# Moving the decode state updates of a gated linear attention from TensorE matmuls in the heads to VectorE multiply-adds in the MLPs

## The chip, the cores and the metric

The kernel runs on one core of one Trainium2 chip. The metric is the device time of one execution in microseconds, and the median of three runs is compared. What counts is the whole step, from the first load to the last output.

## The reference, cut to what matters

One inference step of a two-layer decoder: 256 prompt tokens and 8 decode sequences of 8 new tokens (320 rows together), width 2048, float32. Layer 0 mixes tokens with a gated linear attention (GLA) of 4 heads (keys 256, values 512), layer 1 with a spatial gating unit (gMLP). Each is followed by a layer norm and by a dense MLP of width 8192 with a squared ReLU, and by another layer norm. The part that the change touches is the new state of each decode sequence and head, an output of its own:

```python
def step(s, inp):                     # one chunk; for a decode sequence: its 8 tokens
    qi, ki, vi, gi = inp
    b = jnp.cumsum(gi, axis=-2)
    b_last = b[..., -1:, :]
    k_to_end = ki * jnp.exp(b_last - b)
    ...
    s_new = (jnp.exp(b_last[..., 0, :])[..., None] * s
             + jnp.einsum('bhsk,bhsv->bhkv', k_to_end, vi))
    return s_new, o                   # o uses the old s
def sq_relu_mlp(x, w1, w2):
    return jnp.square(jax.nn.relu(x @ w1)) @ w2
x = layer_norm(ALPHA * x + mixer(x), ...)
x = layer_norm(ALPHA * x + sq_relu_mlp(x, ...), ...)
```

There are 32 such states (8 sequences by 4 heads), each 256 by 512 in float32 (512 KB). Nothing else in the step reads `s_new`.

## The kernel before, in words

**Units.** All activations stand transposed in SBUF, features on partitions, 320 token columns. Every large product goes through `group` (line 165), which walks weight *units* of 512 input rows by 256 output columns. `unit` (line 129) loads a unit (512 KB) on SyncE's queue, ScalarE rounds it to `wh` (line 144, "cast") and VectorE subtracts to get the rest `wl` (line 145, "split"); `mm3` (lines 158 to 163) then issues three matmuls of 320 columns for each of 4 row blocks and 2 column blocks, 24 per unit. Units alternate between two rings of buffers, `a` (4 buffers) and, once the heads are done, `b` (4 buffers, line 712), so a cast waits until TensorE has finished the unit that had its buffer, 8 units earlier. There are 736 units: 24 in each of 4 heads, 32 for the GLA output product, 256 for the first MLP, 64 and 32 for the gMLP layer, 256 for the second MLP.

**Heads.** `Head` (lines 343 to 674) projects v, k, q and the gate of one head, and runs the attention in steps that are spread over the units (`Side`). `ev_v` (line 469) and `ev_k` (line 423) lay each decode token out in four copies of rounded parts and rests, which vector transposes and small gathers (GpSimd's queue, line 341) bring into row order. `sample_step` (line 620) takes one sequence and one half of the keys: two matmuls for the outputs with the old state (line 631), one matmul `pu` of k by v (line 634, 512 columns), and on VectorE `st = st * dec + pu` (line 635); after the second half GpSimd's queue stores the state (line 638). The old state is loaded on SyncE's queue (line 612).

**Norms.** `residual_gemm` (line 853) adds a product to the residual `z` and takes the statistics in `Norm.take` (line 758). The sums over partitions are two pairs of matmuls with a matrix of ones (`total`, lines 754 and 755); `close` (line 801) turns them into mean and `rstd` (lines 806 to 808, and `rsqrt`, lines 186 to 190), and `apply` (line 812) normalises the 16 feature tiles: VectorE lines 816 and 817, ScalarE lines 819 and 820, VectorE line 822 for the rest `yl`. `gemm_of` (line 842) starts the next product on the raw residual `dgh`, `dgl` (two column groups, 8 units, corrected afterwards), so that TensorE needs the first normalised tile only 8 units after the residual product has ended.

**MLPs.** `mlp` (line 875) runs four times a product with `w1`, squared ReLU (VectorE lines 887 and 889, ScalarE lines 888 and 893), and a product with `w2` (VectorE line 908). 

**Order.** Each engine runs its own instructions strictly in the order in which they were built. That order is not the order of the code alone: the program is built with a scheduler that places each instruction on its engine as soon as it reckons its inputs ready, within the buffers that the pools have.

Of the kernel before, what the change touches and what calls it, by code (L numbers as in the profile page):

```python
# [8 lines left out]
F32 = mybir.dt.float32  # L9
F32R = mybir.dt.float32r  # L10
# [65 lines left out]

@with_exitstack
def step_kernel(ctx: ExitStack, tc: tile.TileContext, A):
# [44 lines left out]
    cp.tile([P, LINE - 8], F32, tag="fill", name="fill")  # L123
# [159 lines left out]
    kz = gp.tile([P, 4, 2, 2, P], F32R, tag="kz", name="kz")  # L283
    nc.gpsimd.memset(kz[:].bitcast(F32), 0.0)

# [57 lines left out]
    class Head:  # L343
# [25 lines left out]
        def gate_logits(hd):  # L369

            hd.dec = g2.tile([P, 2, NCH + DB], F32, tag="dec", name=nm("dec"))
# [51 lines left out]
        def ev_k(hd, kt, ps):  # L423
# [12 lines left out]
            kst = g2.tile([P, DB, 4, DS], F32, tag="vst", name=nm("kst"))  # L436
            two = [P, DB, 2, DS]
            hi = kst[:, :, 0:2, :]
            nc.scalar.copy(hi.bitcast(F32R), bc4(kte[:, TP:T]).to_broadcast(two))
            nc.vector.tensor_sub(kst[:, :, 2:4, :], bc4(kte[:, TP:T]).to_broadcast(two), hi)  # L440
# [8 lines left out]
        def gather_kz(hd, q):  # L449
            kb = hd.kb[:].rearrange("p a b -> p (a b)")  # L450
            gather(kz[:, q].bitcast(F32).rearrange("p k b f -> p (k b f)"), kb[:, 2 * TP :], q, nc.gpsimd)
# [17 lines left out]
        def ev_v(hd, vt, ps):  # L469
# [5 lines left out]
            two = [P, DB, 2, DS]  # L475
            hi = vst[:, :, 0::2, :]
            nc.scalar.copy(hi.bitcast(F32R), bc4(ps[:, TP:T]).to_broadcast(two))
            nc.vector.tensor_sub(vst[:, :, 1::2, :], bc4(ps[:, TP:T]).to_broadcast(two), hi)
# [141 lines left out]
        def sample_step(hd, b, kt):  # L620
# [9 lines left out]
            for part in (stl, sth):  # L630
                nc.tensor.matmul(po[:], qm[:, kt, b * P : (b + 1) * P], part[:], start=False,  # L631
                                 stop=(b == DB - 1 and kt == 1 and part is sth))
            pu = gltile()
            nc.tensor.matmul(pairs(pu), kz[:, i, kt, g, :], hd.v_sample(g), start=True, stop=True)  # L634
            nc.vector.scalar_tensor_tensor(st[:, kt, :], st[:, kt, :], hd.dec[:, kt, NCH + b : NCH + b + 1],
                                           pu[:], op0=ALU.mult, op1=ALU.add)
            if kt == 1:
# [516 lines left out]
```

## Time and profile before

| what | value |
|---|---|
| median of 3 runs | 2691.23 us (2691.22 to 2691.33) |
| span of the profiled execution | 2689.4 us, 1.8 us under the median: what lies around the span |
| TensorE busy | 2680.7 us |
| VectorE busy | 1550.3 us (58%) |
| ScalarE busy | 1162.5 us (43%) |
| GpSimd busy | 226.4 us (8%) |
| granted TensorE clock, mean | 1.000 |
| DMA | 442.42 MB, 165 GB/s on average |

Matmuls are pipelined: a matmul of 320 columns shows 0.31 us from its start to its end, but the next one starts 0.14 us later. Busy shares of TensorE therefore say that it never stopped, and what an extra matmul costs is read from starts, not from durations. The heads end about 445 us into the span; the first MLP runs from about 545 to 1430 us, the second from about 1780 to 2667 us.

### The profile page before, as it was taken

The page shows a single profiled execution, that of the slowest core. Times are in us where ns is not written, and L with a number is a line of the kernel's source. Part 1 is how long each engine was busy: PE and PEld are TensorE (multiplying, and loading weights), DVE is VectorE, ACT ScalarE, POOL GpSimd, SP SyncE. Part 2 cuts the span into 40 slices and gives each one's busy share as a digit, 9 for nine tenths or more (in the row PEclk, how much of TensorE's full clock was granted, in tenths as well). Part 3 has the DMA queues.
Part 4 walks back from the last instruction along what each step waited for, and adds up shares of the span by engine and source line. Part 5 has one row for each costly group of instructions (what it writes and reads, how often), then busy time and mean ns, then how long its engine had stood idle before and what let it go on. Part 6 is the DMA issues. An engine that isn't in the chain of part 4 may idle for free.

```text
span 2689.4 us, 44906 instructions
## 1 busy us (share of the span) xinstructions
PE 2680.7 (100%) x18395; PEld 2658.8 (99%) x18395; DVE 1550.3 (58%) x2322; ACT 1162.5 (43%) x1638; POOL 226.4 (8%) x391
## 2 busy tenths in 40 slices
PE   9999999999999999999999999999999999999999
PEld 9999999999999999999999999999999999999998
DVE  7677677885444444444478776686444444444446
ACT  5455455564334334333446554355334333333434
POOL 4353341000000000000001032000000000000000
PEclk9999999999999999999999999999999999999999
DMA  8667667545445545444445555455445444454552
GB/s 252 220 196 249 217 198 253 189 142 159 155 150 155 151 150 156 150 153 152 150 152 161 157 158 149 134 165 153 153 150 156 150 152 154 150 155 150 152 154 79
DMA packets 138494, 442.42 MB, mean 165 GB/s; under 512 B 20912, under 2 KB 27952, under 8 KB 138288
## 3 DMA queue, kind: packets, MB, share of 16 engines
q1 hardware_dynamic: 121440, 408.08, 49.2%
q0 software_dynamic: 16304, 30.82, 3.7%
q8 instruction: 144, 2.36, 0.4%
q10 hardware_dynamic: 544, 0.66, 0.1%
q14 instruction: 62, 0.51, 0.1%
HBM read 409.60 MB, written 22.02 MB: 160 GB/s over the span
## 4 chain that ended last, share of the span: by engine, by line
PE 99%; DMA 0%; ACT 0%; DVE 0%; ACTq 0%; issue 0%; DVEq 0%
PE mm L161 32%; PE mm L163 32%; PE mm L162 31%; PE gl L631 1%; PE gl L634 1%; PE gl L589 1%; PE gl L1003 0%; PE gl L573 0%; DMA raw<-gla_w_in 0%; ACT z L1087 0%; DMA xr<-xT 0%; PE gl L558 0%; PE gl L603 0%; PE gl L574 0%; PE gl L552 0%; PE gl L1004 0%
## 5 line engine op out<-in xcount | busy, mean ns | idle before, releaser
L145 DVE TENSOR_TENSOR wl<-raw,wh 128x1024 fp32r<-128x1024 f32 (+1 forms) x740 | 902.3, 1220 | 953.2 <-ACT wh L144 950.9
L144 ACT CAST wh<-raw 128x1024 fp32r<-128x1024 f32 (+1 forms) x740 | 771.5, 1044 | 1251.9 <-PE mm L163 1127.1
L163 PE MATMUL mm<-yh,wh 128*128 128x320 f32 x2624 | 805.9, 307 | 0.0
L161 PE MATMUL mm<-yh,wl 128*128 128x320 f32 x2624 | 803.2, 309 | 0.0
L162 PE MATMUL mm<-yl,wh 128*128 128x320 f32 x2624 | 794.9, 303 | 0.0
L161 PE MATMUL mm<-hh,wl 128*128 128x320 f32 x2048 | 631.5, 308 | 0.0
L163 PE MATMUL mm<-hh,wh 128*128 128x320 f32 x2048 | 629.0, 307 | 0.0
L162 PE MATMUL mm<-hl,wh 128*128 128x320 f32 x2048 | 619.9, 303 | 0.0
L162 PEld LDWEIGHTS mm<-yl,wh 128*128 128x128 f32 x2624 | 492.7, 188 | 0.0
L163 PEld LDWEIGHTS mm<-yh,wh 128*128 128x128 f32 x2624 | 491.4, 187 | 0.0
L161 PEld LDWEIGHTS mm<-yh,wl 128*128 128x128 f32 x2624 | 491.0, 188 | 0.0
L161 PEld LDWEIGHTS mm<-hh,wl 128*128 128x128 f32 x2048 | 384.6, 188 | 0.0
L162 PEld LDWEIGHTS mm<-hl,wh 128*128 128x128 f32 x2048 | 384.6, 188 | 0.0
L163 PEld LDWEIGHTS mm<-hh,wh 128*128 128x128 f32 x2048 | 383.4, 187 | 0.0
L161 PE MATMUL mm<-xh,wl 128*128 128x320 f32 x768 | 238.2, 311 | 1.4 <-DVE wl L145 0.7
L163 PE MATMUL mm<-xh,wh 128*128 128x320 f32 x768 | 236.4, 309 | 0.0
L162 PE MATMUL mm<-xl,wh 128*128 128x320 f32 x768 | 235.2, 306 | 0.0
L161 PEld LDWEIGHTS mm<-xh,wl 128*128 128x128 f32 x768 | 144.1, 188 | 5.4 <-DVE wl L145 1.0
L162 PEld LDWEIGHTS mm<-xl,wh 128*128 128x128 f32 x768 | 144.3, 188 | 4.4 <-issue 1.2
L163 PEld LDWEIGHTS mm<-xh,wh 128*128 128x128 f32 x768 | 143.7, 187 | 2.6 <-issue 0.7
L1053 POOL CAST ident_r<-ident 128x128 fp32r<-128x128 f32 x1 | 0.3, 286 | 1027.9 <-PE gl L772 1027.9
L936 POOL DMA_DIRECT2D bsp<-sg_wT x1 | 0.6, 558 | 999.7 <-PE mm L163 999.7
(265 smaller groups left out, 2380.3 us busy)
## 6 DMA issues: line engine op xcount, KB each, us to landing
raw<-mlp_w SPq DMA_DIRECT2D x512, 512.0 KB, 3.5
raw<-gla_w_in SPq DMA_DIRECT2D x94, 512.0 KB, 4.1
raw<-sg_w_in SPq DMA_DIRECT2D x64, 512.0 KB, 3.6
st<-state SPq DMA_DIRECT2D x32, 512.0 KB, 5.7
o_state_s<-st POOLq DMA_DIRECT2D x32, 512.0 KB, 4.2
raw<-gla_w_out SPq DMA_DIRECT2D x32, 512.0 KB, 4.5
raw<-sg_w_out SPq DMA_DIRECT2D x32, 512.0 KB, 3.5
va<-blk POOLq DMA_DIRECT2D x128, 32.0 KB, 4.3
```

What stands on the lines that cost most here:

```text
L144: nc.scalar.copy(hi[:, ks, :], raw[:, ks, :])
L145: nc.vector.tensor_sub(lo[:, ks, :], raw[:, ks, :], hi[:, ks, :].bitcast(F32))
L161: nc.tensor.matmul(ps, wl[:, kk, s], x_h, start=first, stop=False)
L162: nc.tensor.matmul(ps, wh[:, kk, s], x_l, start=False, stop=False)
L163: nc.tensor.matmul(ps, wh[:, kk, s], x_h, start=False, stop=last)
L589: nc.tensor.matmul(pairs(pu), hd.ktp[:, kt, blk, :], hd.v_prompt(blk), start=(blk == 0), stop=(blk == 1))
L631: nc.tensor.matmul(po[:], qm[:, kt, b * P : (b + 1) * P], part[:], start=False, stop=(b == DB - 1 and kt == 1 and part is sth))
L634: nc.tensor.matmul(pairs(pu), kz[:, i, kt, g, :], hd.v_sample(g), start=True, stop=True)
L936: nc.gpsimd.dma_start(wsT, A["sg_wT"])
L1053: nc.gpsimd.tensor_copy(ident_r[:], ident[:])
```

## The change

The state update leaves the heads. The one matmul per step, its VectorE instruction, the store, and the row-ordered copies of k (`kz`, with their gathers) are gone; the load of the old state stays, since the outputs need it. Instead the kernel keeps the scaled keys (`ks_all`) and decays (`dec_all`) of all heads in SBUF, writes v of the decode tokens to DRAM (`v_dram`, 16 issues on GpSimd's queue), and computes the states in the MLPs, 16 in each: GpSimd's queue loads the old state again into the only buffer `su` (line 856 of the new file), ScalarE scales its two halves by the decay (line 862), and for each of 8 tokens a row of v (2 KB) is read from DRAM into all 128 partitions (`vt`, two buffers, 256 KB, line 851), and VectorE runs two multiply-adds `su = vt * ks + su` over 128 by 512 (line 872). After the eighth token GpSimd's queue stores the state (line 875). `Spread` is to spread these steps over the MLP's units in the code. Ring `b` has 3 buffers instead of 4.

```diff
+class Spread:
+    def __init__(self, steps, units):
+        self.steps, self.units, self.done, self.called = list(steps), units, 0, 0
+    def __call__(self):
+        self.called += 1
+        while self.done < len(self.steps) and self.done * self.units < self.called * len(self.steps):
+            self.steps[self.done]()
+            self.done += 1
...
+    ks_all = cp.tile([P, H, 2, DB * DS], F32, tag="ks", name="ks_all")
+    dec_all = cp.tile([P, H, 2, NCH + DB], F32, tag="dec", name="dec_all")
+    v_dram = dr.tile([H, 2, P, 4, P], F32, tag="v", name="v_dram")
-    kz = gp.tile([P, 4, 2, 2, P], F32R, tag="kz", name="kz")
-    nc.gpsimd.memset(kz[:].bitcast(F32), 0.0)
...
-            nc.scalar.copy(hi.bitcast(F32R), bc4(kte[:, TP:T]).to_broadcast(two))
-            nc.vector.tensor_sub(kst[:, :, 2:4, :], bc4(kte[:, TP:T]).to_broadcast(two), hi)
+            nc.scalar.copy(ks_all[:, hd.h, kt, :], kte[:, TP:T])
-            nc.vector.transpose(hd.kb[:, 2 + kt, :], kst[:].rearrange("p b c t -> p (b c t)"))
-            if kt == 1:
-                for q in range(4):
-                    hd.gather_kz(q)
...
+            for g in range(2):
+                nc.gpsimd.dma_start(v_dram[hd.h, g, :, 2 * i : 2 * i + 2, :], hd.va[:, i, 1, :, g, :])
...
-            pu = gltile()
-            nc.tensor.matmul(pairs(pu), kz[:, i, kt, g, :], hd.v_sample(g), start=True, stop=True)
-            nc.vector.scalar_tensor_tensor(st[:, kt, :], st[:, kt, :], hd.dec[:, kt, NCH + b : NCH + b + 1],
-                                           pu[:], op0=ALU.mult, op1=ALU.add)
-            if kt == 1:
-                nc.gpsimd.dma_start(SO[b, hd.h].rearrange("(k p) v -> p k v", p=P), st[:])
...
-        wb = ctx.enter_context(tc.tile_pool(name="wb", bufs=4))
+        wb = ctx.enter_context(tc.tile_pool(name="wb", bufs=3))
...
+        def row(h, b, t):
+            vt = l2.tile([P, 6, P], F32, tag="vt", name=nm("vr"))
+            nc.gpsimd.dma_start(vt[:, 0:4, :], v_dram[h, b // 4, 32 * (b % 4) + 2 * DS + t].partition_broadcast(P))
+            cur["next"] = vt
+        def begin(h, b):
+            cur["st"] = l2.tile([P, 2, DV], F32, tag="su", name=nm("su"), bufs=1)
+            nc.gpsimd.dma_start(cur["st"][:], S0[b, h].rearrange("(k p) v -> p k v", p=P))
+        def decay(h, b):
+            st = cur["st"]
+            row(h, b, 0)
+            for kt in range(2):
+                nc.scalar.activation(st[:, kt, :], st[:, kt, :], AF.Identity,
+                                     scale=dec_all[:, h, kt, NCH + b : NCH + b + 1])
+        def token(h, b, t):
+            st, vt = cur["st"], cur["next"]
+            if t + 1 < DS:
+                row(h, b, t + 1)
+            v = vt[:, 0:4, :].rearrange("p a f -> p (a f)")
+            c = b * DS + t
+            for kt in range(2):
+                nc.vector.scalar_tensor_tensor(st[:, kt, :], v, ks_all[:, h, kt, c : c + 1], st[:, kt, :],
+                                               op0=ALU.mult, op1=ALU.add)
+            if t == DS - 1:
+                nc.gpsimd.dma_start(SO[b, h].rearrange("(k p) v -> p k v", p=P), st[:])
...
+        todo = [(h, b) for h in range(H) for b in range(DB)]
+        half = len(todo) // 2
+        up = Spread(updates(todo[i * half : (i + 1) * half]), (2 * NC_ * (D // UN) - 4) * NU)
...
-                gemm(w1, 0, c * D, yh, yl, evict)
+                gemm(w1, 0, c * D, yh, yl, evict, side=up)
```

The scheduler does not leave the steps where `Spread` puts them in the code. In the built program the first multiply-add of the first MLP's 16 states stands in VectorE's queue behind the split of unit 117 (still in the GLA output product), the last behind that of unit 253, half-way through that MLP; those of the second MLP stand from unit 454 (in the gMLP's products) to unit 594. Three places show what moved. Line numbers of the new file are up to 47 higher.

On TensorE, the first MLP's opening, before: the sums of the norm (`gl`, from `lo` and `hi`) among the matmuls on the raw residual (`dgh`, `dgl`).

```order
L163 MATMUL mm_6129<-dgh_5225,wh_6218 128x322
L754 MATMUL gl_6102<-lo_6099,ones_r 128x320
L755 MATMUL gl_6102<-hi_6098,ones_r 128x320
...
L754 MATMUL gl_6109<-lo_6106,ones_r 128x320
L755 MATMUL gl_6109<-hi_6105,ones_r 128x320
L163 MATMUL mm_6130<-dgh_5225,wh_6218 128x322
```

The same place now:

```order
L757 MATMUL gl_5821<-lo_5818,ones_r 128x320
L758 MATMUL gl_5821<-hi_5817,ones_r 128x320
L185 MATMUL mm_5850<-dgh_4944,wh_6129 128x322
L757 MATMUL gl_5828<-lo_5825,ones_r 128x320
L758 MATMUL gl_5828<-hi_5824,ones_r 128x320
L183 MATMUL mm_5851<-dgh_4944,wl_6130 128x322
...
L185 MATMUL mm_5851<-dgh_4944,wh_6129 128x322
L183 MATMUL mm_6234<-yh_5833,wl_6238 128x320
L184 MATMUL mm_6234<-yl_5834,wh_6237 128x320
```

Counted in matmuls on weights, the second sum stood 2.58 units after the residual product's last matmul; now it stands 7.50 units after it, 12 matmuls ahead of the first one that needs a normalised tile (`yh`, `yl`). In the second MLP's opening it moved from 2.58 to 7.79 units after, 5 matmuls ahead. In the three other norms it stands where it stood.

On VectorE, the same norm from behind the variance to the first `yl`, before:

```order
L187 TENSOR_SCALAR nw_6122<-m_920_6116 128x320
L145 TENSOR_TENSOR wl_6579<-raw_6577,wh_6578 128x1024
L188 TENSOR_TENSOR nw_6122<-nw_6122,ny_6123 128x320
L189 TENSOR_TENSOR nw_6122<-nw_6122,ny_6123 128x320
L190 SCALAR_TENSOR_TENSOR rstd_6118<-nw_6122,ny_6123 128x320
L817 SCALAR_TENSOR_TENSOR t_6163<-t_6163,vec,rstd_6118 128x320
L817 SCALAR_TENSOR_TENSOR t_6169<-t_6169,vec,rstd_6118 128x320
L817 SCALAR_TENSOR_TENSOR t_6205<-t_6205,vec,rstd_6118 128x320
L145 TENSOR_TENSOR wl_6609<-raw_6607,wh_6608 128x1024
L822 TENSOR_TENSOR yl_6115<-z,yh_6114 128x320
```

The same now:

```order
L209 TENSOR_SCALAR nw_5841<-m_844_5835 128x320
L167 TENSOR_TENSOR wl_6480<-raw_6478,wh_6479 128x1024
L872 SCALAR_TENSOR_TENSOR su_7328<-vr_7628,ks_all,su_7328 128x512 x2
L210 TENSOR_TENSOR nw_5841<-nw_5841,ny_5842 128x320
L872 SCALAR_TENSOR_TENSOR su_7328<-vr_7666,ks_all,su_7328 128x512 x2
L211 TENSOR_TENSOR nw_5841<-nw_5841,ny_5842 128x320
L212 SCALAR_TENSOR_TENSOR rstd_5837<-nw_5841,ny_5842 128x320
L872 SCALAR_TENSOR_TENSOR su_7328<-vr_7730,ks_all,su_7328 128x512 x2
L820 SCALAR_TENSOR_TENSOR t_5882<-t_5882,vec,rstd_5837 128x320
L820 SCALAR_TENSOR_TENSOR t_5888<-t_5888,vec,rstd_5837 128x320
L820 SCALAR_TENSOR_TENSOR t_5924<-t_5924,vec,rstd_5837 128x320
L825 TENSOR_TENSOR yl_5834<-z,yh_5833 128x320
```

Six multiply-adds stand between the variance and the first `yl`, and two more ahead of line 209 (the row of token 5, directly behind three rows of line 819); one split less does. In the second MLP's opening none stands in this stretch.

On VectorE, later in the first MLP, before: eight units bring 8 splits and the evictions of two column groups, and nothing else.

```order
L145 TENSOR_TENSOR wl_9121<-raw_9119,wh_9120 128x1024
L145 TENSOR_TENSOR wl_9151<-raw_9149,wh_9150 128x1024
L145 TENSOR_TENSOR wl_9181<-raw_9179,wh_9180 128x1024
L887 SCALAR_TENSOR_TENSOR f_8973<-mm_8849,r_8971 128x320
L889 TENSOR_TENSOR hl_8436<-f_8973,hh_8435 128x320
L887 SCALAR_TENSOR_TENSOR f_8979<-mm_8850,r_8977 128x320
L145 TENSOR_TENSOR wl_9211<-raw_9209,wh_9210 128x1024
L889 TENSOR_TENSOR hl_8436<-f_8979,hh_8435 128x320
```

The same place now, from the last token of one state to the first of the next:

```order
L872 SCALAR_TENSOR_TENSOR su_12011<-vr_12413,ks_all,su_12011 128x512 x2
L167 TENSOR_TENSOR wl_9035<-raw_9033,wh_9034 128x1024
L932 SCALAR_TENSOR_TENSOR f_8879<-mm_8746,r_8877 128x320
L934 TENSOR_TENSOR hl_8303<-f_8879,hh_8302 128x320
L932 SCALAR_TENSOR_TENSOR f_8885<-mm_8747,r_8883 128x320
L167 TENSOR_TENSOR wl_9133<-raw_9131,wh_9132 128x1024
L934 TENSOR_TENSOR hl_8303<-f_8885,hh_8302 128x320
L167 TENSOR_TENSOR wl_9103<-raw_9101,wh_9102 128x1024
L872 SCALAR_TENSOR_TENSOR su_12514<-vr_12576,ks_all,su_12514 128x512 x2
```

One whole state (16 multiply-adds) now stands in every 8 units, and between two states VectorE has three splits and four evictions queued. On GpSimd's queue the store of a state is followed by one row, then by the load of the next state, which waits for that store since both use `su`.

More of the change, by code (lines that the diff above doesn't have):

```diff
@@ L74, in flush @@
             self.steps.pop(0)()
+class Spread:
[6 more added lines that the diff above has]
+            self.done += 1
+    def flush(self):
+        while self.done < len(self.steps):
+            self.steps[self.done]()
+            self.done += 1
 @with_exitstack
@@ L840, in gemm, with updates, gemm_of @@
             i += n2
-    def gemm_of(norm, out, w, col0, evict_raw, evict):
+    def updates(todo):
+        cur = {}
+        def row(h, b, t):
[22 more added lines that the diff above has]
+                nc.gpsimd.dma_start(SO[b, h].rearrange("(k p) v -> p k v", p=P), st[:])
+        for h, b in todo:
+            yield lambda h=h, b=b: begin(h, b)
+            yield lambda: None
+            yield lambda h=h, b=b: decay(h, b)
+            for t in range(DS):
+                yield lambda h=h, b=b, t=t: token(h, b, t)
+    def gemm_of(norm, out, w, col0, evict_raw, evict, later=None):
         yh, yl = parts(out, "y")
@@ L849, in gemm_of @@
         for i in range(2, D // UN):
[L850 removed]
+            group(w, 0, (col0 + i * UN,), yh, yl, lambda n, ps, i=i: evict(2 * i + n, ps), later)
         return yh, yl
```

28 lines of the change are left out of this document (12 added, 16 removed).

## The prediction

> **What bounds the kernel now.** I read the page first (span, engines, the chain that ended last), then the waits, then single stretches of the timeline.
>
> ```profile
> span 2689.4 us, 44906 instructions
> PE 2680.7 (100%) x18395; PEld 2658.8 (99%) x18395; DVE 1550.3 (58%) x2322; ACT 1162.5 (43%) x1638; POOL 226.4 (8%) x391
> PE 99%; DMA 0%; ACT 0%; DVE 0%; ACTq 0%; issue 0%; DVEq 0%
> PE mm L161 <- DVE wl L145: 0.7, 1, 0.7
> ```
>
> TensorE never stops: 8.7 us of the span are not its own, the chain is its, and of the waits on weights the one that the trace lists is 0.7 us long, once. So a matmul taken out of any stretch shortens the step, and any wait that reaches TensorE lengthens it. What stands between is the lead with which weights are made ready. The timeline of ScalarE and VectorE in the first MLP shows it:
>
> ```profile
> 702.73 1.05 ACT L144 CAST wh<-raw 128x1024 fp32r<-128x1024 f32 x1 [2.42 <-PE mm L163]
> 706.20 1.05 ACT L144 CAST wh<-raw 128x1024 fp32r<-128x1024 f32 x1 [2.42 <-PE mm L163]
> ...
> 703.82 1.23 DVE L145 TENSOR_TENSOR wl<-raw,wh 128x1024 fp32r<-128x1024 f32 x1 [2.24 <-ACT wh L144]
> ```
>
> A cast starts every 3.47 us, each time when TensorE frees a buffer: that is TensorE's time for a unit (24 matmuls of 0.144 us), and the rings are full. From cast to end of split is 2.3 us. With 8 buffers a unit is cast when TensorE finishes the 8th before it, and is used 7 units later: a lead of 24.3 - 2.3 = 22 us.
>
> **The change, part by part.**
>
> *The matmul that goes.* The timeline in a head:
>
> ```profile
> 89.33 0.39 PE L634 MATMUL gl<-va,kz 128*128 128x512 f32 x1
> 89.56 0.31 PE L161 MATMUL mm<-xh,wl 128*128 128x320 f32 x1
> 89.71 0.31 PE L162 MATMUL mm<-xl,wh 128*128 128x320 f32 x1
> ...
> L634 PE MATMUL gl<-va,kz x64: 388/394/800, 84.5 to 432.2; 128*128 128x512 f32 x64
> ```
>
> Durations overlap; starts count. The next start is 0.23 us later (a 320-column one, 0.15). 64 x 0.23 = **14.8 us** off TensorE, on the path. The VectorE update, the copies of k, 64 gathers and 32 stores in the heads go too, worth nothing: TensorE covers them. The v rows' 16 stores to DRAM stand on GpSimd's queue ahead of k's gathers, which are wanted only late in the head: nothing, and about one landing of 3 to 4 us per head on that queue, still hidden, were they wanted at once.
>
> *Ring b of 3.* Units alternate, so a unit in b now waits for the 6th before it: the lead falls by 6.9 to **15 us**. By itself it costs nothing (0.7 us of waits on splits in all, above); it is the cushion for what follows.
>
> *VectorE's new work.* Rows that group it, and three starts in a dense stretch:
>
> ```profile
> L145 DVE TENSOR_TENSOR wl<-raw,wh 128x1024 fp32r<-128x1024 f32 x734 | 899.4, 1226 | 950.1 <-ACT wh L144 947.9
> L635 DVE SCALAR_TENSOR_TENSOR st<-st,dec,gl 128x512 f32<-128x512 f32 x64 | 45.8, 742 | 20.1 <-PE gl L634 19.8
> L628 ACT CAST sth<-st 128x512 fp32r<-128x512 f32 x64 | 37.8, 619 | 22.8 <-PE gl L631 19.4 <-DMA st<-state 2.9
> 561.76 1.22 DVE L145 TENSOR_TENSOR wl<-raw,wh 128x1024 fp32r<-128x1024 f32 x1
> 562.89 0.49 DVE L822 TENSOR_TENSOR yl<-z,yh 128x320 fp32r<-128x320 f32 x1
> 563.30 0.49 DVE L816 TENSOR_TENSOR t<-nd,z 128x320 f32<-128x320 f32 x1
> ```
>
> From start to start a queued split takes 1.13 us and a 320-column operation 0.41, some 0.08 under their durations. The multiply-add isn't in the trace; nearest is L635 (same shape, scalar per partition): 0.742 long, so 0.66 in a dense queue, and 0.72 by its busy time over its count. I take 0.70 for it, 1.15 for a split and 0.45 for an eviction. A state is 16 x 0.70 = 11.2 us, all of one MLP's 179 us. Were it spread over the MLP's 887 us it would vanish in VectorE's idle half. But the built order packs one state into every 8 units (27.7 us), and VectorE may not pass over an instruction that waits.
>
> *The loop of one state.* Landings (the line with three numbers is that of the 32 stores, L638) and a dependent issue:
>
> ```profile
> st<-state SPq DMA_DIRECT2D x32, 512.0 KB, 5.7
> o_state_s<-st POOLq DMA_DIRECT2D x32, 512.0 KB, 4.2
> vt<-bsp POOLq DMA_DIRECT2D x64, 24.0 KB, 3.1
> bsp<-sg_wT POOLq DMA_DIRECT2D x1, 512.0 KB, 4.3
> bsp<-sg_bs POOLq DMA_DIRECT2D x1, 512.0 KB, 6.4
> DMA to landing us min/median/max: 3.1/4.2/8.1
> 1463.97 0.55 POOL L939 DMA_DIRECT2D bsp<-sg_bs  x1
> 1470.67 0.56 POOL L942 DMA_DIRECT2D bsp<-sg_wT  x1 [1.94 <-DMA bsp<-sg_bs]
> ```
>
> From a landing (1463.97 + 6.4) to the issue that waited for it: 0.3 us. With one buffer `su`, from the last token of a state to the first of the next: store 4.2, load 5.0 (between 4.3 alone on this queue and 5.7 behind weights), half the decay on ScalarE 0.6 (L628), three hand-overs of 0.3: **10.7 us**. VectorE's queue holds three splits and four evictions there (two behind `w2`), 5.2 us; then it stands, and behind it every split that TensorE needs. Rows of v: two buffers, so row t+2 is issued when token t is done and lands 3.7 us later (between 3.1 for 24 KB and 4.3 for 512 KB). Token 2 can start 1.4 + 0.3 + 3.7 = 5.4 us after token 0 started, while two tokens and a split take 3.95: it waits 1.4, later tokens 0.4 together. The loop: 10.7 + 11.2 + five splits 5.75 + four evictions 1.8 + rows 1.8 = 31.2 us behind `w1`, 30.3 behind `w2`. TensorE wants 27.7: **3.0 us too long** on average. About 11 states per MLP stand in this pattern (those from unit 160 and from unit 510 on): 33 us, less the lead of 15, = 18 per MLP, **36 us** in all. Bounds: store 3.1 (the shortest of these 32), load 4.3, rows 3.1 and multiply-adds of 0.66 give 28.4 and 27.4, nothing that reaches TensorE; load 5.7, rows 5.0 (the trace's only broadcast, `sg_bs`, twice as large, took 6.4) and 0.74 give about 36 us, 2 x (11 x 8 - 15) = 146.
>
> Trainium skill, DMA: Bandwidth & Descriptors, section Anatomy of one DMA: it fits a GpSimd-issued DMA as 2.0 us + bytes / 436 GB/s, by estimate 3.2 us for a state and 2.6 for a row. The rows here are longer (4.2 and 4.3 for 512 KB). By the page the loop would be 27.0 us and this term zero, the step 2705.
>
> *The norm's opening.* Here the order moved most. Before, in the first MLP:
>
> ```profile
> 553.39 0.43 ACT L806 ACTIVATE m<-gl 128x320 f32<-128x320 f32 x1
> 557.52 0.56 ACT L186 ACTIVATE ny<-m,eps_l 128x320 f32<-128x320 f32 x1
> 561.04 0.56 ACT L819 ACTIVATE yh<-t,vec 128x320 fp32r<-128x320 f32 x1
> ...
> 554.76 0.31 PE L755 MATMUL gl<-hi,ones_r 128*128 128x320 f32 x1
> 574.12 0.31 PE L161 MATMUL mm<-yh,wl 128*128 128x320 f32 x1
> ```
>
> From the second sum to the end of the first `yl` (562.89 + 0.49, above) is 8.6 us, and TensorE asks for it only 19.4 us after the sum. Now only 12 matmuls (1.7 us) stand between sum and use, and in the second MLP 5 (0.7 us). In the first, eight multiply-adds more and one split less stand in the chain: 8.6 + 5.6 - 1.15 = 13.1, a stall of 11.3; in the second 8.6 - 0.7 = 7.9. Then the other 15 tiles come slower: 16 multiply-adds stand among them in the first, 19 in the second, 11 and 13 us; TensorE's order leaves it later groups to do meanwhile, so I count 5 each. Openings: **29 us**. Bounds: no multiply-add in the way, 6.9 + 7.9 = 15; all in the way, 19 + 24 = 43.
>
> *ScalarE* gets 64 decays of 0.6 us, covered by its idle half; a decay that waits for its load holds the casts behind it, but these casts' splits stand behind the same state's first token, so that is in the loop. *DMA*: per 8 units 7.3 MB instead of 4.2, 265 GB/s at full pace. The page's slices:
>
> ```profile
> GB/s 252 220 196 249 217 198 253 189 142 159 155 150 155 151 150 156 150 153 152 150 152 161 157 158 149 134 165 153 153 150 156 150 152 154 150 155 150 152 154 79
> ```
>
> The heads (the first six or seven) went up to 253; hence landings from the heads' rows.
>
> **Sum.** 2691.2 - 14.8 + 36 + 29 = **2741 us** (the profiled execution's span lies 1.8 under the median of 2691.2, and is shortened or lengthened by the same terms).
>
> **The rivals.**
>
> *Loop hidden.* If landings are short enough for a loop of 27.7 us, only the openings cost: 2691.2 - 14.8 + 29 = 2705. For it: the smallest landings in the rows. Against it: 265 GB/s wanted. The Trainium skill's fit for DMAs, above, gives this case.
>
> *The clock falls.* The end of the trace by windows (PE, PEld, DVE, ACT, POOL busy, then the granted clock):
>
> ```profile
> 2680.00:2684.00 4.00, 3.20 (x22) 2.94 (x20) 4.00 (x10) 4.00 (x10) 3.35 (x5) 1.00 0.88 313
> 2684.00:2688.00 4.00, 0.00 (x0) 0.00 (x0) 0.15 (x1) 0.74 (x2) 0.00 (x0) 0.89 0.89 319
> ```
>
> When TensorE stands still the granted clock drops. If it comes back at half speed for half a unit after each of some 24 waits, that is 24 x 1.7 = 41 us more: 2782. It decides only where waits are long; those of 3 us may be too short. Trainium skill, TensorE: Matmul & The Clock Gate, Part 1: after an idle window of about 3.4 us the array runs at half clock until it was busy for about as long. The 0.89 agrees in kind; by the page both openings would pay, about 3.4 us in all, and the waits between states perhaps.
>
> *Faster.* The 14.8 us stay if the openings' stall is under 14.8. Part of the 8.6 us was VectorE's own queue; what must follow each other is a sum (0.31), ScalarE (0.43, 0.56, twice 0.56) and seven operations on VectorE of 0.41 to 0.5: 5.4, with six hand-overs of 0.1 (my estimate) 6 us. Then the stalls are 4.3 and 5.3, and with the loop hidden and the other tiles in time the step takes 2686 or a little less. It decides where the chain takes less than 8.6 us in both MLPs with no multiply-add in its way. Against it: eight of them stand in the first, on record in the order.
>
> *It does not do what it says.* The order places the states in half of each MLP, not spread over it; that is already in the sum.
>
> **How the numbers follow.** Forecast (both terms) 0.55, loop hidden 0.20, clock or landings beyond 2780 0.12: slower, 0.87. Faster by over 0.2% (5.4 us, about what a measurement of this kernel can tell) 0.07; in between, with openings near 15 and no loop, 0.06. The range runs from openings at their lower bound, 2691 (rounded down to 2690), to 2820, where the loop costs 115 instead of 36.
>
> **What would show it.** Right: TensorE idle near 574 and 1810 us of the span, some 10 us each, ended by `yh` or `yl`; then waits on splits in the half of each MLP that holds the states, and none in the other half; VectorE idle some 5 us per state, ended by ScalarE's decay, whose own wait ends with the load of `su`. Wrong: TensorE at 100% through the states, or a multiply-add far from 0.70 us, or rows that land in under 3 us.

## The result, and the profile after

The changed kernel takes 2870.0 us (median of 4, 2865.1 to 2871.6) against 2691.2 us: a ratio of 1.066 (95% interval 1.065 to 1.068). The forecast of slower was right; the size was not: 179 us where 50 were forecast, and 2870 lies outside the range. The page of the changed kernel (the span, the busy times, the chain that ended last, the landings):

```profile
span 2869.9 us, 45885 instructions
...
PE 2721.8 (95%) x18331; PEld 2687.4 (94%) x18331; DVE 1826.1 (64%) x2754; ACT 1190.3 (41%) x1718; POOL 363.5 (13%) x630
...
PE 61%; DMA 15%; DVE 11%; issue 10%; POOL 1%; ACT 1%; DVEq 0%; ACTq 0%; POOLq 0%
...
L872 DVE SCALAR_TENSOR_TENSOR su<-vr,ks_all,su 128x512 f32<-128x512 f32 x512 | 364.3, 747 | 176.0 <-DMA vr<-v_dram 109.6
...
raw<-mlp_w SPq DMA_DIRECT2D x512, 512.0 KB, 3.7
vr<-v_dram POOLq DMA_DIRECT2D x256, 256.0 KB, 4.1
...
su<-state POOLq DMA_DIRECT2D x32, 512.0 KB, 5.9
o_state_s<-su POOLq DMA_DIRECT2D x32, 512.0 KB, 4.8
```

The chain was TensorE's to 99%; now 61% is. DMA, VectorE and issue have the rest. The multiply-adds are as short as forecast (364.3 us for 512, 0.71 each), and VectorE waited 110 us for rows ahead of them. What TensorE waited for (in the kernel before its only wait on a split was one of 0.7):

```profile
PE mm L183 <- DVE wl L167: 68.9, 34, 7.5
PE mm L183 <- ACT yh L822: 27.0, 3, 15.8
PE mm L183 <- ACT hh L933: 14.9, 2, 10.2
PE gl L798 <- DVE a L796: 10.8, 1, 10.8
```

Windows of the changed kernel, cut where the matmuls on weights reach units 128, 160, 254, 464, 512 and 596 (busy PE, PEld, DVE, ACT, POOL, then granted clock, DMA share, GB/s):

```profile
531.50:673.10 141.60, 120.05 (x773) 117.57 (x773) 123.12 (x203) 69.77 (x118) 21.98 (x38) 0.90 0.65 206
673.10:1074.00 400.90, 347.43 (x2258) 341.66 (x2257) 247.71 (x324) 118.03 (x150) 60.16 (x104) 0.94 0.66 204
1074.00:1817.80 743.80, 743.80 (x5172) 743.76 (x5171) 444.13 (x679) 320.62 (x453) 60.90 (x103) 1.00 0.51 160
1817.80:2023.90 206.10, 178.42 (x1160) 174.91 (x1159) 180.98 (x296) 103.60 (x166) 28.13 (x49) 0.93 0.64 204
2023.90:2366.80 342.90, 308.98 (x2017) 304.89 (x2017) 222.80 (x292) 107.37 (x137) 52.75 (x92) 0.96 0.70 213
```

The third window holds no state until 1746 us, then one and the start of the next, and TensorE is at 100% in it. The others are the openings and the packed states, at 0.90 to 0.96 of the clock. The same units in a kernel without states (e_none, below) take 112.3, 325.8, 743.8, 167.9 and 291.2 us. So the openings of the MLPs cost 29 and 25 us (in the fourth window 13 more fall to the end of the gMLP's output product, units 464 to 480, where the middle sum of the norm, line 798, comes late), and the packed states 75 and 52.

One gap between two states in the changed kernel, from the last token of one to the first of the next (VectorE, ScalarE, GpSimd's queue):

```profile
898.63 1.41 DVE L872 SCALAR_TENSOR_TENSOR su<-vr,ks_all,su 128x512 f32<-128x512 f32 x2 [0.41 <-DMA vr<-v_dram]
...
905.71 1.22 DVE L167 TENSOR_TENSOR wl<-raw,wh 128x1024 fp32r<-128x1024 f32 x1
914.38 2.74 DVE L872 SCALAR_TENSOR_TENSOR su<-vr,ks_all,su 128x512 f32<-128x512 f32 x4 [7.45 <-ACT su L862]
...
904.39 1.05 ACT L166 CAST wh<-raw 128x1024 fp32r<-128x1024 f32 x1
913.62 1.34 ACT L862 ACTIVATE su<-su,dec_all 128x512 f32<-128x512 f32 x2 [8.18 <-DMA su<-state]
...
900.34 0.72 POOL L875 DMA_DIRECT2D o_state_s<-su  x1 [2.81 <-DVE su L872]
901.06 0.55 POOL L851 DMA_DIRECT2D vr<-v_dram  x1
906.43 0.71 POOL L856 DMA_DIRECT2D su<-state  x1 [4.82 <-DMA o_state_s<-su]
```

Token, store, load, decay, token, one after the other, as forecast; VectorE stands for 7.45 us, ScalarE for 8.18. Over all gaps the mean is 12.7: 0.3 to the store's issue, 5.0 for its landing, 0.3, 5.9 for the load's, 1.1 until the first token.

### The profile page after: what moved, and what is told of

It reads as the page before. It is cut to its first block, busy times and chain, and to the rows that moved or that the text cites. A ratio compares the mean times of both kernels' runs of the same rounds, so it can differ in the third digit from the quotient of the medians.

```text
span 2869.9 us, 45885 instructions
## 1 busy us (share of the span) xinstructions
PE 2721.8 (95%) x18331; PEld 2687.4 (94%) x18331; DVE 1826.1 (64%) x2754; ACT 1190.3 (41%) x1718; POOL 363.5 (13%) x630
## 4 chain that ended last, share of the span: by engine, by line
PE 61%; DMA 15%; DVE 11%; issue 10%; POOL 1%; ACT 1%; DVEq 0%; ACTq 0%; POOLq 0%
PE mm L183 20%; PE mm L185 19%; PE mm L184 19%; DMA vr<-v_dram 9%; DVE su L872 5%; DMA su<-state 4%; DVE wl L167 3%; DMA raw<-mlp_w 1%; PE gl L640 1%; POOL o_state_s L875 1%; POOL vr L851 0%; PE gl L598 0%; DMA raw<-sg_w_out 0%; ACT wh L166 0%; ACT su L862 0%
## 5 line engine op out<-in xcount | busy, mean ns | idle before, releaser
L166 ACT CAST wh<-raw 128x1024 fp32r<-128x1024 f32 (+1 forms) x740 | 761.7, 1043 | 1292.7 <-DMA raw<-mlp_w 585.9
L183 PE MATMUL mm<-yh,wl 128*128 128x320 f32 x2624 | 816.0, 313 | 68.3 <-DVE wl L167 37.6
L185 PE MATMUL mm<-yh,wh 128*128 128x320 f32 x2624 | 815.0, 311 | 0.0
L184 PE MATMUL mm<-yl,wh 128*128 128x320 f32 x2624 | 806.3, 308 | 7.9 <-DVE yl L825 7.7
L183 PE MATMUL mm<-hh,wl 128*128 128x320 f32 x2048 | 641.4, 313 | 45.7 <-DVE wl L167 30.7
L184 PE MATMUL mm<-hl,wh 128*128 128x320 f32 x2048 | 628.8, 307 | 4.0 <-DVE hl L934 4.0
L183 PEld LDWEIGHTS mm<-yh,wl 128*128 128x128 f32 x2624 | 500.1, 191 | 74.2 <-DVE wl L167 42.1
L185 PEld LDWEIGHTS mm<-yh,wh 128*128 128x128 f32 x2624 | 499.9, 191 | 0.0
L872 DVE SCALAR_TENSOR_TENSOR su<-vr,ks_all,su 128x512 f32<-128x512 f32 x512 | 364.3, 747 | 176.0 <-DMA vr<-v_dram 109.6
L851 POOL DMA_DIRECT2D vr<-v_dram x256 | 138.7, 542 | 790.4 <-DVE su L872 732.9
```

Of the source, the lines that this page charges most:

```text
L166: nc.scalar.copy(hi[:, ks, :], raw[:, ks, :])
L183: nc.tensor.matmul(ps, wl[:, kk, s], x_h, start=first, stop=False)
L184: nc.tensor.matmul(ps, wh[:, kk, s], x_l, start=False, stop=False)
L185: nc.tensor.matmul(ps, wh[:, kk, s], x_h, start=False, stop=last)
L851: nc.gpsimd.dma_start(vt[:, 0:4, :], v_dram[h, b // 4, 32 * (b % 4) + 2 * DS + t].partition_broadcast(P))
L872: nc.vector.scalar_tensor_tensor(st[:, kt, :], v, ks_all[:, h, kt, c : c + 1], st[:, kt, :], op0=ALU.mult, op1=ALU.add)
```

## The experiments

Three theories were set against each other. **Theory A**, the prediction's: each engine's order is fixed, the order gives a state a slot of so many units, and what a state costs is its real loop less that slot. **Theory B**: the weights' own chain is what slows, since a raw buffer (3 of them) comes free only after a split that may stand behind a waiting multiply-add. **Theory C**: the added work itself, 364 us of VectorE and the transfers, crowds out the weights. (A cast reads a weight unit from its raw buffer into the rings, a split follows it.) The runs are gathered here. "Tokens" is from the first multiply-add of a state to its last, "gap" from there to the next state's first, "loop" their sum (means over the last 10 loops of each MLP, from starts and ends of the multiply-adds); "slot" is the number of splits in between, by 3.467 us; "idle" is TensorE's, summed over the gaps between its instructions from 450 us to 12 us ahead of the end; "loss" is the profiled span over that of e_none, 2674.5.

| run | us | tokens + gap = loop | slot | loop - slot | idle | loss |
|---|---|---|---|---|---|---|
| changed kernel | 2870.0 | 22.7 + 12.8 = 35.5 | 28.8 | 6.7 | 140 | 195 |
| b_ring3 | 2692.6 | | | | | |
| e_none | 2674.0 | | | | 2 | 0 |
| e_spread | 2718.8 | 23.1 + 29.8 = 52.9 | 52.0 | 0.9 | 32 | 46 |
| e_open | 2904.9 | 22.8 + 13.5 = 36.4 | 27.7 | 8.6 | 162 | 226 |
| e_ring2 | 3020.2 | 24.9 + 12.2 = 37.1 | 30.7 | 6.4 | 240 | 344 |
| e_raw4 | 2884.9 | 22.4 + 12.6 = 35.0 | 28.4 | 6.5 | 147 | 209 |
| e_su2 | 3018.4 | 27.2 + 1.7 = 28.8 | 23.1 | 5.8 | 237 | 342 |
| e_half | 2861.8 | 18.6 + 12.6 = 31.2 | 23.4 | 7.8 | 124 | 186 |
| e_slot9 | 2830.6 | 23.0 + 13.8 = 36.8 | 31.2 | 5.6 | 109 | 154 |
| e_slot9s | 2796.1 | 23.3 + 12.6 = 35.9 | 31.2 | 4.7 | 86 | 120 |
| e_slot10 | 2804.1 | 22.5 + 16.6 = 39.1 | 34.7 | 4.4 | 89 | 128 |
| e_slot10r | 2723.8 | 18.5 + 17.5 = 36.0 | 34.7 | 1.3 | 30 | 48 |
| e_row3 | 2781.0 | 19.3 + 12.8 = 32.1 | 28.8 | 3.3 | 77 | 105 |
| e_best | 2674.0 | 33.0 + 16.7 = 49.7 | 49.9 | -0.3 | 0 | -3 |

Loop less slot is a way of counting: it says by how much the splits of a state came later than at TensorE's full pace, and not what made them late. What shows a cause is what an edit does to it, and to the time.

b_ring3, e_none, e_spread, e_open and e_best were timed four times or more, the others once. Times of one kernel lie up to 10 us apart here (e_open), so of the single times only differences of 30 us and more are read.

**One part alone: the ring of 3** (the kernel before, with one number changed).

```diff
-        wb = ctx.enter_context(tc.tile_pool(name="wb", bufs=4))
+        wb = ctx.enter_context(tc.tile_pool(name="wb", bufs=3))
```

> The kernel before with nothing changed but ring b, 3 buffers instead of 4. First theory (the loop of one state is what costs; the ring is only a cushion): 2691 us, no change, since TensorE never waited for a split with a lead of 22 us and should not with 15. Rival (the shorter ring itself costs): 2700 us or more, with TensorE waits for wl in the MLPs.

Ratio 1.0004 (0.9995 to 1.0013): nothing, as expected.

**The removal alone** (an empty list of states, so that `o_state_s` stays unwritten).

```diff
-        up = Spread(updates(todo[i * half : (i + 1) * half]), ...)
+        up = Spread((), ...)
```

> The changed kernel without any state update in the MLPs (no loads, rows, multiply-adds or stores there; o_state_s stays unwritten). It measures the removal from the heads with the ring of 3. First theory: 2674 us, the 17 us that the heads became shorter in the profile of the change, and no wait of TensorE in the MLPs. Rival (the ring of 3, or the rest of the change in the heads, costs by itself): 2690 us or more.

2674.0 us, ratio 0.9938 (0.9923 to 0.9953): the removal is worth 17.1 us. All the rest, 196 us, is what the states cost in the MLPs.

**The same instructions, spread.** `issue_after` puts an instruction behind a given one in its engine's order; it adds no wait.

```diff
+            last["cast"] = nc.scalar.copy(hi[:, ks, :], raw[:, ks, :]).ins        # in unit()
...
+            with tc.issue_after(last["cast"]):                                    # in decay()
                 for kt in range(2):
                     nc.scalar.activation(st[:, kt, :], ...)
```

> The changed kernel with the same instructions, but the decay of each state may not be issued before the cast of the unit at which the code calls it, so a state takes 15 units of 52 us instead of 8 of 27.7 us and none lies in an opening. First theory (a loop of about 35 us in a slot of 27.7 us): the loop fits, 2674 to 2682 us, faster than the kernel before. Rival (the added work itself, 364 us of VectorE and the transfers, crowds out splits and raw loads wherever it stands): 2800 us or more.

2718.8 us. With every multiply-add, row, load and store in place the loss falls from 196 to 45 us, so Theory C is out as the main cause: it is where the work stands. My 2674 to 2682 was missed as well; TensorE still waited 14 times, 32 us in all, most of it in four groups:

```profile
PE mm L185 <- DVE yl L826: 12.6, 5, 4.4
PE gl L799 <- DVE a L797: 8.9, 2, 5.1
PE mm L184 <- ACT hh L935: 4.4, 2, 3.6
PE mm L185 <- DVE hl L936: 3.2, 2, 2.4
```

None of the four is a wait for weights themselves. They are the short chains at which TensorE has nothing else to do: a `yl` of an opening, the middle sum of a norm, the last `hh` and `hl` ahead of a change from `w1` to `w2`. In the openings and in the wait for `hl` that ends at 1111 us multiply-adds stand among the operations of such a chain. But in the waits that end at 1339, 1393 and 2648 us (12.5 of the 32) no multiply-add stands in the 10 us before: a cast that waits for its raw load holds up what TensorE needs. ScalarE, ahead of the first two:

```profile
1337.23 1.04 ACT L167 CAST wh<-raw 128x1024 fp32r<-128x1024 f32 x1 [4.29 <-DMA raw<-mlp_w]
1387.77 2.00 ACT L167 CAST wh<-raw 128x1024 fp32r<-128x1024 f32 x2 [4.70 <-DMA raw<-mlp_w]
```

So a part of what e_spread still loses is the weights' own chain, with no multiply-add in it.

**The openings free of multiply-adds, the states still packed.**

```diff
+            def scaled():                                                         # in decay(): the two activations
+                ...
+            if (h, b) == todo[0]:
+                with tc.issue_after(last["cast"]):
+                    scaled()
+            else:
+                scaled()
```

> The changed kernel with only the first state of each MLP held back to the place where the code calls it; the other 15 still follow it packed, 8 units each, so the openings are free of multiply-adds and the loops run on 4 or 5 states longer behind them. First theory (the loop is too long by 7 us a state wherever it stands, and the openings pay the same excess): 2674 + 2 x (16 x 6.9 - 15) = 2865 us. Rival (the openings are a cost of their own, the norm chain displaced by multiply-adds): 2870 - 54 - 13 = 2803 us.

2904.9 us, above both. The total alone would mislead. With the windows cut at the same units and held against e_none, the openings cost 11 and 11 us instead of 29 and 25, and the middle sum nothing instead of 13; the packed states (here units 160 to 280 and 512 to 624) cost 207 instead of 127. So the openings are a cost of their own, as the rival has it, but the states moved out of them cost more behind them (loop less slot 8.6).

**The weights' chain: rings, raw buffers, state tiles** (SBUF has room for the last two only where ring b gives a buffer up, so e_ring2 is their control).

```diff
-        wb = ctx.enter_context(tc.tile_pool(name="wb", bufs=3))
+        wb = ctx.enter_context(tc.tile_pool(name="wb", bufs=2))                   # all three
-    wraw = ctx.enter_context(tc.tile_pool(name="wraw", bufs=3))
+    wraw = ctx.enter_context(tc.tile_pool(name="wraw", bufs=4))                   # e_raw4
-            cur["st"] = l2.tile([P, 2, DV], F32, tag="su", name=nm("su"), bufs=1)
+            cur["st"] = l2.tile([P, 2, DV], F32, tag="su", name=nm("su"), bufs=2) # e_su2
```

> The changed kernel with ring b of 2 buffers instead of 3, the control for the next two. Both theories: one ring buffer is 7 us of lead, lost once in each MLP, so about 14 us more than the changed kernel, 2884 us.

> As e_ring2, with 4 raw buffers for weights instead of 3. Theory A (the state's own loop of store, load, decay and 8 rows takes 34 us in a slot of 27.7): the same as e_ring2 within 10 us. Theory B (the weights' chain: a raw buffer comes free only after a split, which stands behind a waiting multiply-add, so casts wait 586 us for raw loads): clearly less, 2780 us or below.

> As e_ring2, with two state tiles instead of one, so that the next state is loaded while the one before is still computed and stored; the order now gives a state 7 units, 24.3 us. Theory A: the gap of 14 us between two states shrinks to about 1 us, the loop to some 24 us, so the packed states cost little: 2674 + 54 for the openings + 14 for the ring, about 2740 us (2720 to 2790). Theory B: the rows and splits stay as they are, 2850 us or more.

The control was a bad one: 3020 us, not 2884. Most of the 150 us more fall where no state is near (units 280 to 384 take 410 us instead of 361). There, in e_ring2 (ScalarE, VectorE, SyncE's queue):

```profile
1252.66 2.00 ACT L166 CAST wh<-raw 128x1024 fp32r<-128x1024 f32 x2 [5.42 <-DMA raw<-mlp_w]
1253.74 2.36 DVE L167 TENSOR_TENSOR wl<-raw,wh 128x1024 fp32r<-128x1024 f32 x2 [5.06 <-ACT wh L166]
1254.99 16.18 SPq L160 DMA_DIRECT2D raw<-mlp_w  x6
```

Casts come in pairs after a wait for a load, and the loads are issued when the splits are done. The order says why: with rings of 4 and 2 ScalarE's casts run ahead in the larger ring (raw tiles 13688, 13868, 13770, 13950, 13834, where the loads go 13688, 13722, 13770, 13804, 13834, 13868, 13916, 13950), so three raw buffers hold tiles that are wanted out of turn and none is loading ahead. A fourth raw buffer (e_raw4) takes 135 us of that away, which is the case of neither theory (within 10 us of e_ring2 for A, 2780 us or below for B). But it does not touch the packed states: their units (160 to 254 and 512 to 596) cost 125 us over e_none in e_ring2, 134 in e_raw4 and 127 in the changed kernel. So Theory B is a real effect of unequal rings, and not what the packed states of the changed kernel paid, as far as this pair tells; a fourth raw buffer beside a ring of 3 had no room, and rings of equal size were not run. In e_su2 the gap is gone (1.7 us), but the order shrank the slot to 23.1 us in return, and the loop, now mostly tokens, is 28.8: 5.8 us per state again. Its time is the one named for Theory B (2850 us or more); since the slot moved with the loop, the run does not tell the two apart.

**Half of the multiply-adds.**

```diff
-            for kt in range(2):
+            for kt in range(1):                                                   # in token()
                 nc.vector.scalar_tensor_tensor(st[:, kt, :], v, ...)
```

> The changed kernel with the multiply-adds of the first half of each state's rows alone (kt 0; the other half of each state is only decayed), so half the added VectorE work, 182 us less, all transfers as they were; the order then gives a state 6.6 units, 23 us, instead of 8. Theory A (each state costs what its store, load and rows really take beyond the slot, about 6 us, whatever its multiply-adds): 2674 + 32 x 6 = 2866 us. Rival C (the added VectorE time is what crowds the splits): half of the excess goes, 2772 us.

2861.8 us, near Theory A's 2866 and far from 2772. Half of the added work on VectorE is gone, and the time is 8 us less, no more than times of one kernel differ by: the order shortened the slot (28.8 to 23.4) by about what was taken out. That the total agrees with Theory A's is partly luck: the openings cost 26 us instead of 54, the packed states 152 instead of 127 (loop less slot 7.8, where about 6 was expected).

**The slot set by hand** (as e_spread, with another number of units).

```diff
-        up = Spread(updates(todo[i * half : (i + 1) * half]), (2 * NC_ * (D // UN) - 4) * NU)
+        up = Spread(updates(todo[i * half : (i + 1) * half]), half * 9)           # e_slot10: half * 10
```

> As e_spread, with the decays held at 9 units a state instead of 15 (a slot of 31.2 us). Theory A (a loop really takes 34 to 35 us; what a state costs is the loop less its slot): 2719 as e_spread + 32 x 3.4 = about 2828 us. Rival (the added VectorE time and transfers crowd the weights; the slot only says where): the same loss on a longer stretch, 2870 us or more.

> As e_slot9, with 10 units a state (34.7 us). Theory A: the slot is as long as the loop, so the states cost nearly nothing beyond e_spread, 2719 to 2735 us. Rival: 2860 us or more.

2830.6 us for 9 units, 2 us from Theory A's number, but by luck: the loop came out at 36.8 instead of 34 to 35, so loop less slot was 5.6 and not 3.4, and by the same sum, 2719 + 32 x 5.6, the time would have been 2898. 10 units gave 2804.1, neither 2719 to 2735 nor the rival's 2860, since the loop became 39.1. Its gap in e_slot10 (VectorE, then ScalarE, then GpSimd's queue):

```profile
929.59 2.36 DVE L168 TENSOR_TENSOR wl<-raw,wh 128x1024 fp32r<-128x1024 f32 x2 [5.95 <-ACT wh L167]
935.52 1.23 DVE L168 TENSOR_TENSOR wl<-raw,wh 128x1024 fp32r<-128x1024 f32 x1 [3.57 <-ACT wh L167]
936.66 2.07 DVE L874 SCALAR_TENSOR_TENSOR su<-vr,ks_all,su 128x512 f32<-128x512 f32 x3
...
934.44 1.05 ACT L167 CAST wh<-raw 128x1024 fp32r<-128x1024 f32 x1 [3.92 <-DMA raw<-mlp_w]
935.39 1.33 ACT L864 ACTIVATE su<-su,dec_all 128x512 f32<-128x512 f32 x2
...
925.49 0.71 POOL L857 DMA_DIRECT2D su<-state  x1 [4.33 <-DMA o_state_s<-su]
```

The state had landed at 930.95 (925.49 and 5.46 for its landing), but the decay stands behind a cast that waits for its raw load. On average the decay starts 4.2 us after its load has landed; in the changed kernel it was 0.1. So Theory B's chain does enter, by the decay: the more units stand in the gap, the more raw loads the loop goes through. A loop is no constant that a longer slot can simply outgrow.

**The rows** (a third row buffer, 2 KB, fits beside a ring of 3).

```diff
-            vt = l2.tile([P, 6, P], F32, tag="vt", name=nm("vr"))
+            cur["n"] = (cur.get("n", -1) + 1) % 3
+            vt = l2.tile([P, 6, P], F32, tag="vt", name=nm("vr")) if cur["n"] else l2.tile([P, 4, P], F32, tag="vr", name=nm("vr"), bufs=1)
```

> The changed kernel, packed as it is (8 units a state), with a third row buffer, so that a row is loaded one token earlier. If the rows' landing of 4.1 us is the part of the loop that I priced too low (110 us of waits of multiply-adds for rows, 3.4 us a state): the loop falls to 31 us and the time to about 2870 - 110 = 2760 us. If the gap between two states (store 4.8, load 5.9, and what stands between) sets it: 2850 us or more.

> As e_slot10 (10 units a state, 34.7 us, whose loop turned out as 39 us), with a third row buffer. If the rows' landing is a term of the loop by itself, the 8 multiply-adds take some 4 to 5 us less as in e_row3, the loop is 34 to 35 us, no longer than its slot, and the states cost little: 2719 to 2740 us. If the loop is held by something else that fills its slot whatever its parts are: 2790 us or more.

2781.0 us for the changed kernel with this one edit: 89 us gained of the 110 expected. The multiply-adds' waits for rows fell from 109.6 us (92 times) to

```profile
DVE su L873 <- DMA vr<-v_dram: 10.2, 17, 1.9
```

and the tokens of a state from 22.7 to 19.3 us, in the same slot. In e_slot10r the loop fell from 39.1 to 36.0 and the time from 2804 to 2723.8, inside the expected 2719 to 2740, although the gap stayed at 17.5. In e_row3 the slot is the same 28.8 and the openings are no cheaper (36 and 25 us), but the packed states cost 45 us instead of 127: of all edits to the changed kernel as it is packed, this is the one that shows a term of the loop by itself.

**The store.**

```diff
-            if t == DS - 1:
+            if t == DS - 1 and (h, b) == todo[-1]:
                 nc.gpsimd.dma_start(SO[b, h]...)
```

> As e_slot9 (9 units a state, 31.2 us), leaving out all stores of states but the last of each MLP, so that the load of a state waits for no store to land. If the store's landing of 4.8 us stands in the loop by itself: the gap of 13.6 us falls to about 9, the loop from 36.8 to 32 us, and the time from 2831 to 2719 + 32 x 0.8, about 2745 us. If decays stand behind casts and raw loads anyway, the gap stays above 12 us and the time above 2800 us.

2796.1 us against e_slot9's 2830.6, and the gap only 1.2 us shorter, at 12.6. The decay now starts 5.7 us after its load has landed on average, at once in every second state and some 10 us late in the others: the casts ahead of it, which wait for raw loads, take the store's place. The time is just under the 2800 of that case; a store's 5 us are no term that can be taken out alone.

**A version that beats both.** As e_spread, with the multiply-adds held too, and no step in the places where e_spread's TensorE waited.

```diff
     def __call__(self):
+        self.u = getattr(self, "u", 7) + 1
+        if self.u < 16 or self.u % 32 in (30, 31, 0, 1) or 237 <= self.u <= 243:
+            return
         self.called += 1
...
-        up = Spread(updates(...), (2 * NC_ * (D // UN) - 4) * NU)
+        up = Spread(updates(...), 197)
...
+            with tc.issue_after(last["split"]):                                   # in token()
                 for kt in range(2):
                     nc.vector.scalar_tensor_tensor(st[:, kt, :], v, ...)
```

> As e_spread, with decays and multiply-adds held at units that lie outside the openings, outside 4 units around each change of the weights' matrix and outside 7 units around the middle sum of the norm, the places where TensorE waited in e_spread (31 us of waits). Theory A (a multiply-add costs only where TensorE waits for the next short chain of VectorE and ScalarE): 2676 to 2690 us, faster than the kernel before. Rival (the waits move to other evictions, lead being short all through the states): 2700 us or more.

2674.0 us, ratio to the kernel before 0.9937 (0.9920 to 0.9953). Its page:

```profile
span 2671.9 us, 45902 instructions
...
PE 2664.1 (100%) x18331; PEld 2645.8 (99%) x18331; DVE 1822.3 (68%) x2754; ACT 1204.3 (45%) x1718; POOL 364.1 (14%) x630
```

That is e_none's time with all 32 states computed, 2 us below the range of Theory A. The whole work of the change is free; only its order was dear. Two things differ from e_spread, the places kept free and the multiply-adds spread out (tokens 33.0 us instead of 23.1); which of them brought how much of the last 45 us was not separated.

## Why the prediction was right or wrong

- **The matmul that goes**, -14.8: -17.1 measured (e_none). Right in kind and nearly in size; where the other 2.3 us come from stays open.
- **Ring b of 3**, nothing by itself: right alone (b_ring3, 1.4 us with an interval across zero). That it makes the order of casts uneven, and would matter at 2, I did not see.
- **VectorE's new work**, 0.70 us a multiply-add: 0.71. Right, and that it "would vanish in VectorE's idle half" if spread is shown by e_best.
- **The loop of one state**, 36 us: this is the step that failed. The mechanism was the forecast one (the chain of the gap above, e_row3, e_slot10r, e_best), but the terms were too short. The gap was 12.8 us, not 10.7: the store landed in 5.0, not 4.2, the load in 5.9, not 5.0. The store's price came from the heads; the load's lay between one alone on this queue and those of the heads on SyncE's queue; neither was measured on this queue beside the MLPs' stream of weights. The tokens took 22.7, not 20.5: a row landed in 4.1, not 3.7, and the two row buffers turn that into waits again and again (110 us in all). So loop less slot was 6.7 (35.5 against 28.8), not 3.0, and the packed states cost 75 + 52 = 127. That the rows were a term too short is shown by e_row3: loop less slot 3.3, packed states 45. The gap's share is read from the trace alone, since leaving out the store (e_slot9s) did not shorten the gap by its landing. The formula of the prediction, with the measured loop and slot, gives 2 x (11 x 6.7 - 15) = 117; that is no test of it, as both are measured from the same late splits. Being a difference of two nearly equal numbers, the term was off by a factor of 3.5 where the loop was off by some 15%. The bound of 146 held it; the range did not, as it took 115 beside the openings' 29 for the far end and left no room for openings that are dear too.
- **The openings**, 29 us: 54. The stalls were right in kind and place: TensorE waits for `yh` until 576 us (15.8 us, forecast 11.3) and until 1926 (10.4, forecast 7.9). The forecast rightly counted multiply-adds (half of them, in e_half, brought the openings to 26 us), but no waits inside the chain; the trace of the changed kernel has a row that comes late in it, and in the second opening a cast ahead of `yh` that waits 5.3 us for its raw load:

```profile
571.42 1.41 DVE L872 SCALAR_TENSOR_TENSOR su<-vr,ks_all,su 128x512 f32<-128x512 f32 x2 [1.51 <-DMA vr<-v_dram]
575.79 0.56 ACT L822 ACTIVATE yh<-t,vec 128x320 fp32r<-128x320 f32 x1 [9.22 <-DVE t L820]
...
1924.43 1.04 ACT L166 CAST wh<-raw 128x1024 fp32r<-128x1024 f32 x1 [5.26 <-DMA raw<-mlp_w]
```

- **Not priced**: the middle sum of the gMLP's norm, 13 us (line 798 waits 10.8 us). Ahead of it stand four multiply-adds, which the order had placed as early as unit 454, and a cast that waits 5.6 us for its raw load; I had that place on record and gave it no term. With a third row buffer (e_row3) it costs 1 us.
- **The clock**, a rival with 0.12: it came, beside the loop and not in its place. In all runs with waits the loss is 1.37 to 1.58 times TensorE's idle time (195 to 140 in the changed kernel); busy TensorE is 2721.8 us there and 2664.9 in e_none. Of the 127 us of the packed states TensorE stood idle for 87 and was busy 39 longer than in e_none. Its price belonged beside the forecast's waits, not in a case of its own.
- **What would show it** was all seen: idle TensorE near 575 and again in the second opening (at 1925 instead of 1810, as the step was some 100 us late by then), waits on splits in the half of each MLP with states and none in the other (the third window), VectorE held by the decay and the decay by the load.

Sum: -17 + 127 + 54 + 13 + 1 (units 112 to 120) = +178, and 179 was measured. The windows share out the whole span, so this sum has to come out and proves nothing; it says where the time went.

## What to carry to other kernels

Work that would fit an engine's idle half costs nothing only if the order leaves it room: compare the real loop of the moved work (with every landing read beside the traffic that it will meet) with the slot that the built order gives it, count the buffers through which it is fed (one row buffer more took 89 us off), and expect an order that is built from estimates to shrink the slot when the work shrinks. Hold such work back to a pace that leaves slack, and keep it out of the short chains where the bounding engine has nothing else to do; that turned +179 us into -17. Where the forecast is a small difference of two long times, let the range follow the error of the long ones.

## What the runs showed of the hardware

A wait of TensorE can cost more than its length. After the wait of 2.88 us that ends at 740.57 in the changed kernel, the matmuls start 0.15 us apart for one microsecond, then 0.27 for 3.2 us:

```profile
740.57 0.42 PE L183 MATMUL mm<-hh,wl 128*128 128x320 f32 x1 [2.88 <-DVE wl L167]
740.82 0.31 PE L184 MATMUL mm<-hl,wh 128*128 128x320 f32 x1
740.97 0.31 PE L185 MATMUL mm<-hh,wh 128*128 128x320 f32 x1
...
742.07 0.47 PE L185 MATMUL mm<-hh,wh 128*128 128x320 f32 x1
742.33 0.47 PE L183 MATMUL mm<-hh,wl 128*128 128x320 f32 x1
```

The window in that slow part (busy times of the engines, then the granted clock, 0.51):

```profile
743.00:745.00 2.00, 2.00 (x10) 2.00 (x9) 1.35 (x3) 0.00 (x0) 0.54 (x1) 0.51 0.64 242
```

Of eleven other waits in that stretch those of 2.7 and 3.2 us had such a slow part behind them and those of 0.4 to 1.9 none; of three between 2.2 and 2.6 one had. The length does not decide it alone: further on a wait of 1.8 us (ending at 1065.43) had one behind it, and one of 2.9 us (2251.64) none. The Trainium skill, TensorE: Matmul & The Clock Gate, Part 1, says that the array runs at half clock after an idle window of about 3.4 us until it was busy as long; the trace agrees on the half and on the length of the slow part, and has it after shorter waits.

A broadcast row of 256 KB landed in 4.1 us and a state of 512 KB in 4.8 (store) and 5.9 (load), medians of the changed kernel, while the windows with states moved 204 to 213 GB/s. The Trainium skill, DMA: Bandwidth & Descriptors, section Anatomy of one DMA, would give by estimate 2.6 and 3.2; the trace disagrees, by 1.5 us for a row and by 1.6 and 2.7 for a state.
